# A dilated 3x3 convolution: scheduler-made streams replaced by hand-written engine streams, with a loop on TensorE

## The chip, the cores and the metric

The kernel runs on one core of a Trainium2 chip. The metric is the device time of one execution in microseconds (us): 127.39 us before the change, the median of three runs (127.07, 127.39 and 127.62 us).

## The reference

Each of 16 images has 64 input channels of 64 x 64 pixels and gives 128 output channels of the same size. The kernel is 3 x 3 with dilation 2 and zero padding of 2:

```python
for kh in range(3):
    for kw in range(3):
        output[b, co] += weight[co, ci, kh, kw] * \
            x_pad[b, ci, kh*2 : kh*2 + 64, kw*2 : kw*2 + 64]   # summed over ci
```

Input and output are 32-bit floats: 16.8 MB are read and 33.6 MB are written.

## The kernel before, in words

**Pairs and groups.** Two images (a pair) lie on 128 partitions, 64 channels each, so there are 8 pairs. A pair is worked on in 4 groups of 16 image rows, 32 groups in all, counted by `G`. TensorE multiplies each image with its own 64 rows of the array, so every product is issued twice (`hb`), once for each half.

**Fewer products.** Dilation 2 makes rows of equal `(row // 2) % 2` share terms. For a group, VectorE first adds neighbouring row pairs (`rowsum`, line 85, into `xs`). TensorE then makes three results in PSUM, each of 1024 numbers for each of 128 output channels: `psP`, the middle row of weights on the sums (6 matmuls and 6 weight loads), and `psA` and `psB`, with differences of weights on the single rows (12 each). ScalarE copies `psP` to SBUF (`p_sb`, line 233). VectorE adds `psA + p_sb` and `psB + p_sb` into the output tile `osb` (line 240). So a group has 30 matmuls, one copy, two adds and one row sum, and ScalarE also casts one chunk of the input from 32 to 16 bits (line 73).

**Weights.** At the start the weights are loaded, cast and subtracted on three engines, turned by matmuls against an identity (line 124), and copied to `w_sb`. Dummy matmuls on zeros (line 101) fill TensorE's waits there.

**Transfers.** All of them are issued on SyncE's queue (SP), one after another: weights (line 88), inputs by pair (line 64, 2 MB for a pair), outputs (lines 185 and 191, 4 MB for a pair). SyncE waits in order: a transfer whose data or buffer isn't ready holds all behind it. The order is: weights, pair 0 in two parts, pairs 1, 2, 3, then stores of pair 0, loads of pairs 4 and 5, stores of pair 1, load 6, stores of pair 2, load 7 in two parts, then stores only. Each transfer is divided over the core's 16 DMA engines. There are three input buffers, three 16-bit input buffers, three output buffers, one PSUM buffer for `psP` and three shared by `psA` and `psB`.

**One store is cut unevenly.** In the last pair, 256 KB of one store go out as 124 partitions and 4 partitions (`FOUR`), where the others have 128.

**Order and waits.** The code is written in program order, and the framework (in its manual schedule) keeps that order on each engine and puts in the semaphores. All loops are unrolled: TensorE's stream has 2009 instructions in the built program (each matmul counted with its weight load).

Of the kernel before, what the change touches and what calls it, by code (L numbers as in the profile page):

```python
# [10 lines left out]
def kernel(  # L11
# [31 lines left out]
    XF = 3  # L43

    wpool = ctx.enter_context(tc.tile_pool(name="wpool", bufs=1))
    fpool = ctx.enter_context(tc.tile_pool(name="fpool", bufs=XF))
    xpool = ctx.enter_context(tc.tile_pool(name="xpool", bufs=3))
    sxpool = ctx.enter_context(tc.tile_pool(name="sxpool", bufs=2))
    opool = ctx.enter_context(tc.tile_pool(name="opool", bufs=3))
    spool = ctx.enter_context(tc.tile_pool(name="spool", bufs=3))  # L50
    ppool = ctx.enter_context(tc.tile_pool(name="ppool", bufs=1, space=bass.MemoryType.PSUM))
    apool = ctx.enter_context(tc.tile_pool(name="apool", bufs=3, space=bass.MemoryType.PSUM))
# [4 lines left out]
    ctx.enter_context(tc.manual_schedule())  # L57

    x32_tiles, x16_tiles, xs_tiles, o_tiles = {}, {}, {}, {}

    def load(pb, cuts=(0, H)):
        x32_tiles[pb] = fpool.tile([P, HW], f32, tag="x32", name="x32")
        for lo, hi in zip(cuts[:-1], cuts[1:]):
            nc.sync.dma_start(  # L64
                out=x32_tiles[pb][:, lo * W : hi * W], in_=x_pair[pb, :, lo * W : hi * W]
            )

    def cast(c):
        pb, g = divmod(c, NG)
        lo, hi = chunk_rows[g]  # L70
        if g == 0:
            x16_tiles[pb] = xpool.tile([P, HW], f16, tag="x16", name="x16")
        nc.scalar.copy(  # L73
            out=x16_tiles[pb][:, lo * W : hi * W], in_=x32_tiles[pb][:, lo * W : hi * W]
        )

    def rowsum(c):
        pb, g = divmod(c, NG)
        if g == 0:
            xs_tiles[pb] = sxpool.tile([P, HW // 2], f16, tag="xs", name="xs")  # L80
        v = x16_tiles[pb][:, g * GR * W : (g + 1) * GR * W].rearrange(
            "p (b e q) -> p b e q", e=2, q=2 * W
        )
        s = xs_tiles[pb][:, g * NH : (g + 1) * NH].rearrange("p (b q) -> p b q", q=2 * W)
        nc.vector.tensor_tensor(out=s, in0=v[:, :, 0], in1=v[:, :, 1], op=add)  # L85

    w32 = wpool.tile([CO, CI * KH * KW], f32, name="w32")
    nc.sync.dma_start(out=w32, in_=weight.rearrange("o i h w -> o (i h w)"))  # L88
    load(0, (0, 2 * GR + d, H))
    load(1)  # L90
    load(2)
    zero = wpool.tile([P, 512], f16, name="zero")
    nc.vector.memset(zero, 0.0)  # L93
    ident = wpool.tile([P, P], f16, name="ident")
    make_identity(nc, ident)

    dm = ppool.tile([P, 2 * NH], f32, tag="p", name="dm")

    def dummies(n):
        for _ in range(n):  # L100
            nc.tensor.matmul(out=dm[:, 0:512], lhsT=zero[:, 0:P], rhs=zero)  # L101

    KINDS = 5
    NT = KINDS * KW
    wd = wpool.tile([CO, NT * CI], f16, name="wd")
    wdv = wd.rearrange("o (k j i) -> o k j i", k=KINDS, j=KW)
    wv = w32.rearrange("o (i h w) -> o h w i", h=KH, w=KW)
    w_sb = wpool.tile([P, NT * CO], f16, name="w_sb")

    dummies(6)  # L110
    nc.vector.tensor_copy(out=wdv[:, 0], in_=wv[:, 1])  # L111
    nc.gpsimd.tensor_tensor(out=wdv[:, 3], in0=wv[:, 0], in1=wv[:, 1], op=sub)  # L112
    nc.scalar.copy(out=wdv[:, 2], in_=wv[:, 0])  # L113
    nc.vector.tensor_tensor(out=wdv[:, 1], in0=wv[:, 2], in1=wv[:, 1], op=sub)
    nc.gpsimd.tensor_copy(out=wdv[:, 4], in_=wv[:, 2])  # L115

    wts = [apool.tile([P, 1024], f32, tag="ab", name="wt") for _ in range(3)]

    def turn(k):
        c0 = k // 3 * 512  # L120
        for j in range(KW):
            t = k * KW + j
            for r in range(2):
                nc.tensor.matmul(  # L124
                    out=wts[k % 3][r * CI : (r + 1) * CI, c0 + j * CO : c0 + (j + 1) * CO],
                    lhsT=wd[:, t * CI : (t + 1) * CI],
                    rhs=ident,
                )
        return w_sb[:, k * KW * CO : (k + 1) * KW * CO], wts[k % 3][:, c0 : c0 + KW * CO]

    x16_tiles[0] = xpool.tile([P, HW], f16, tag="x16", name="x16")
    t0 = turn(0)
    dummies(2)
    nc.vector.tensor_copy(out=t0[0], in_=t0[1])
    t1 = turn(1)
    nc.scalar.copy(out=t1[0], in_=t1[1])  # L136
    t2 = turn(2)
    nc.vector.tensor_copy(out=t2[0], in_=t2[1])  # L138
    dummies(1)
    t3 = turn(3)  # L140
    t4 = turn(4)
    dummies(1)
    nc.vector.tensor_copy(
        out=x16_tiles[0][:, 8 * W : 18 * W], in_=x32_tiles[0][:, 8 * W : 18 * W]
    )
    nc.scalar.copy(out=x16_tiles[0][:, 0 : 8 * W], in_=x32_tiles[0][:, 0 : 8 * W])  # L146
    nc.scalar.copy(out=t3[0], in_=t3[1])
    nc.vector.tensor_copy(out=t4[0], in_=t4[1])
    rowsum(0)

    ahead = [1]

    def casts(G):
        for n in range(2 if G else 3):
            c = ahead[0]
            if c >= ngroups or c > G + (7 if c < 2 * NG else 5):
                return
            cast(c)
            ahead[0] += 1

    def product(ps, src, kind, blk0, nblk, first, last):
        for j in (1, 0, 2):
# [3 lines left out]
            for hb in range(2):  # L166
# [4 lines left out]
                nc.tensor.matmul(  # L171
# [5 lines left out]
                )  # L177

    def blocks(x16, b0, n, e):
        v = x16.rearrange("p (b e r w) -> p b e r w", e=2, r=2, w=W)  # L180
        return lambda pp, c0, c1: v[pp, b0 : b0 + n, e, :, c0:c1]

    def store(pb, m, r0=0, r1=H, rows=((0, P),)):
        for lo, hi in rows:
            nc.sync.dma_start(
                out=out_img[2 * pb + m, lo:hi, r0 * W : r1 * W],
                in_=o_tiles[pb][lo:hi, m * HW + r0 * W : m * HW + r1 * W],
            )

    def store_both(pb, r0, r1):  # L190
        nc.sync.dma_start(
            out=out_img[2 * pb : 2 * pb + 2, :, r0 * W : r1 * W].rearrange("m o q -> o m q"),
            in_=o_tiles[pb].rearrange("p (m q) -> p m q", m=2)[:, :, r0 * W : r1 * W],
        )

    FOUR = ((0, P - 4), (P - 4, P))
    ROWS4 = 8

    for G in range(ngroups):
        pb, g = divmod(G, NG)  # L200
        x16 = x16_tiles[pb]
        xs = xs_tiles[pb].rearrange("p (r w) -> p r w", w=W)
        if g == 0:
            o_tiles[pb] = opool.tile([P, 2 * HW], f32, tag="osb", name="osb")
        o = o_tiles[pb].rearrange("p (m b e q) -> p m b e q", m=2, e=2, q=2 * W)
        b0 = g * NBLK

        def summed():
            ps = ppool.tile([P, 2 * NH], f32, tag="p", name="psP")
            sv = lambda pp, c0, c1: xs[pp, g * GR // 2 : (g + 1) * GR // 2, c0:c1]  # L210
            product(ps, sv, 0, 0, NBLK, True, True)
            return ps

        if G:
            psP = summed()

        psA = apool.tile([P, 2 * NH], f32, tag="ab", name="psA")
        product(psA, blocks(x16, b0, NBLK, 1), 1, 0, NBLK, True, False)
        z = 1 if g == 0 else 0
        product(psA, blocks(x16, b0 + z - 1, NBLK - z, 1), 2, z, NBLK - z, False, True)  # L220

        psB = apool.tile([P, 2 * NH], f32, tag="ab", name="psB")
        product(psB, blocks(x16, b0, NBLK, 0), 3, 0, NBLK, True, False)
        z = 1 if g == NG - 1 else 0
        product(psB, blocks(x16, b0 + 1, NBLK - z, 0), 4, 0, NBLK - z, False, True)

        if not G:
            psP = summed()

        if not G:  # L230
            casts(0)
        p_sb = spool.tile([P, 2 * NH], f32, tag="psb", name="p_sb")
        nc.scalar.copy(out=p_sb, in_=psP)  # L233
        if G:
            casts(G)
        if G + 1 < ngroups:
            rowsum(G + 1)
        pv = p_sb.rearrange("p (m b q) -> p m b q", m=2, q=2 * W)
        for e, ps in ((0, psA), (1, psB)):
            nc.vector.tensor_tensor(  # L240
                out=o[:, :, b0 : b0 + NBLK, e],
                in0=ps.rearrange("p (m b q) -> p m b q", m=2, q=2 * W),
                in1=pv,
                op=add,
            )

        if G == 0:
            load(XF)
        if g == NG - 1 and 0 < pb < npairs - XF - 1:
            load(pb + XF + 1, (0, H) if pb < 3 else (0, H // 2, H))  # L250
# [14 lines left out]
        elif g == NG - 1:  # L265
            store(pb, 0)
            store(pb, 1)

# [33 lines left out]
```

## Time and profile before

| | us |
|---|---|
| median of three runs | 127.39 |
| span of the profiled execution, first to last instruction | 125.1 |
| TensorE busy (share of the span) | 104.6 (84%) |
| VectorE busy | 91.0 (73%) |
| ScalarE busy | 65.0 (52%) |
| the transfers of SyncE's queue, as a share of 16 DMA engines' span | 96.5% |
| last matmul row starts | 106.65 |
| last add starts | 108.08 |

The profile is of one execution. Its span is 2.3 us shorter than the median of the runs; the page gives no other time for that execution. The page lists busy time by engine, then the span in 40 equal slices of 3.13 us, then the DMA queues (`q1` carries the kernel's transfers, `q8` fetches of instructions), the chain of work that ended last, and the costliest groups of instructions with the mean time of one and what they waited for. The issues of transfers have their own list: how often, how many KB, and the median time from issue to landing. The trace also holds a record of every DMA packet with its queue, start, size and duration.

### The profile page before, as it was taken

To read this page: it belongs to the slowest core of one execution; us is meant where nothing else is said; L and a number is where in the kernel's file an instruction comes from. 1 tells how busy PE (TensorE), PEld (TensorE's weight loads), DVE (VectorE), ACT (ScalarE), POOL (GpSimd) and SP (SyncE) were. 2 spreads that over 40 slices of the span, in tenths; PEclk is the share of its full clock that TensorE was granted. 3 is DMA by queue.
4 is the path that set the end of the run, shared out by engine and by line. 5 is a ranking of instruction groups with operands and counts; after the bars stand their busy time and mean duration, and the time that the engine had idled before them with its cause. 6 is when DMAs were issued, how large, how long until landed. Compare 5 with 4: busy or idle time off the path is not lost.

```text
span 125.1 us, 2339 instructions
## 1 busy us (share of the span) xinstructions
PE 104.6 (84%) x1000; PEld 56.7 (45%) x1000; DVE 91.0 (73%) x103; ACT 65.0 (52%) x68; POOL 2.2 (2%) x8
## 2 busy tenths in 40 slices
PE   6885999999999999999999999999999999500000
PEld 2342555555555555555555555555555555200000
DVE  0652998988898889888988898887988988700000
ACT  4377896665666566656665666566653333100000
POOL 2400000000000000000000000000000000000000
PEclk9999999999999999999999999999999999965555
DMA  4999999999999999999999999999999999999981
GB/s 123 389 457 430 435 430 419 377 430 397 438 434 430 367 424 424 432 445 419 435 419 404 417 445 435 430 430 435 424 424 424 430 424 440 430 409 411 428 379 66
DMA packets 4594, 50.78 MB, mean 406 GB/s; under 512 B 488, under 2 KB 488, under 8 KB 1256
## 3 DMA queue, kind: packets, MB, share of 16 engines
q1 hardware_dynamic: 4584, 50.63, 96.5%
q8 instruction: 8, 0.13, 0.4%
q14 instruction: 2, 0.02, 0.0%
HBM read 17.07 MB, written 33.55 MB: 405 GB/s over the span
## 4 chain that ended last, share of the span: by engine, by line
PE 76%; DMA 6%; ACT 2%; DVE 1%; DVEq 1%; SPq 1%; issue 0%
PE psA L171 31%; PE psB L171 30%; PE psP L171 16%; DMA x<-in_x_dram 6%; ACT x L73 2%; DVE osb L240 1%; DVEq L300 1%; ACT p_sb L233 1%; SPq L64 0%; SPq L88 0%; DVEq L240 0%
## 5 line engine op out<-in xcount | busy, mean ns | idle before, releaser
L171 PEld LDWEIGHTS <-w_sb 64*128 64x128 f16 x960 | 54.6, 94 | 46.3 <-issue 1.6
L233 ACT COPY p_sb<-psP 128x1024 f32<-128x1024 f32 x32 | 32.4, 1012 | 36.6 <-issue 21.5
L240 DVE TENSOR_TENSOR osb<-psA,p_sb 128x1024 f32<-128x1024 f32 x32 | 39.2, 1225 | 13.5 <-PE psA L171 9.4
L171 PE MATMUL psA<-x,w_sb 64*128 64x496 f16 (+3 forms) x384 | 45.1, 365 | 0.5 <-ACT x L146 0.5
L171 PE MATMUL psB<-x,w_sb 64*128 64x496 f16 (+3 forms) x384 | 45.1, 365 | 0.0
L240 DVE TENSOR_TENSOR osb<-psB,p_sb 128x1024 f32<-128x1024 f32 x32 | 39.1, 1222 | 0.0
L73 ACT CAST x<-x 128x1024 f16<-128x1024 f32 (+2 forms) x31 | 32.1, 1044 | 0.7 <-DMA x<-in_x_dram 0.7
L171 PE MATMUL psP<-xs,w_sb 64*128 64x496 f16 (+1 forms) x192 | 26.0, 371 | 1.3 <-ACT p_sb L233 1.3
L85 DVE TENSOR_TENSOR xs<-x 128x512 f16<-128x512 f16 x32 | 13.3, 416 | 0.7 <-ACT x L73 0.7
L101 PE MATMUL dm<-zero 128*128 128x512 f16 x10 | 4.1, 533 | 1.2 <-DVE zero L93 1.2
L111 DVE CAST wd<-w 128x192 f16<-128x192 f32 x1 | 0.5, 506 | 2.6 <-DMA w<-in_weight_dram 2.6
L101 PEld LDWEIGHTS <-zero 128*128 128x128 f16 x10 | 1.0, 121 | 2.6 <-DVE zero L93 1.2
L124 PEld LDWEIGHTS <-wd 128*64 128x64 f16 x30 | 1.0, 118 | 1.9 <-DVE wd L111 1.3
L124 PE MATMUL wt<-ident,wd 128*64 128x128 f16 x30 | 1.5, 239 | 0.4 <-DVE wd L111 0.4
L113 ACT ACT_TABLE_LOAD x1 | 1.3, 1283 | 0.7 <-PEq L286 0.7
L113 ACT CAST wd<-w 128x192 f16<-128x192 f32 x1 | 0.5, 543 | 1.7 <-DMA w<-in_weight_dram 1.7
L136 ACT CAST w_sb<-wt 128x384 f16<-128x384 f32 x1 | 0.5, 479 | 1.4 <-PE wt L124 1.4
L93 DVE MEMSET zero<- 128x256 uint32 x1 | 0.3, 272 | 0.9 <-PEq L286 0.9
L146 ACT CAST x<-x 128x512 f16<-128x512 f32 x1 | 0.6, 618 | 0.5 <-DMA x<-in_x_dram 0.5
L138 DVE CAST w_sb<-wt 128x384 f16<-128x384 f32 x1 | 0.6, 558 | 0.4 <-PE wt L124 0.4
L112 POOL TENSOR_TENSOR wd<-w 128x192 f16<-128x192 f32 x1 | 0.8, 798 | 2.5 <-DMA w<-in_weight_dram 2.5
L115 POOL CAST wd<-w 128x192 f16<-128x192 f32 x1 | 0.8, 806 | 0.0
(11 smaller groups left out, 3.8 us busy)
## 6 DMA issues: line engine op xcount, KB each, us to landing
out_dram<-osb SPq DMA_DIRECT2D x12, 2048.0 KB, 18.4
x<-in_x_dram SPq DMA_DIRECT2D x6, 2048.0 KB, 16.3
out_dram<-osb SPq DMA_DIRECT2D x4, 1024.0 KB, 13.8
out_dram<-osb SPq DMA_DIRECT2D x2, 1536.0 KB, 12.1
x<-in_x_dram SPq DMA_DIRECT2D x2, 1024.0 KB, 19.4
x<-in_x_dram SPq DMA_DIRECT2D x1, 1088.0 KB, 5.5
x<-in_x_dram SPq DMA_DIRECT2D x1, 960.0 KB, 7.3
out_dram<-osb SPq DMA_DIRECT2D x1, 768.0 KB, 15.5
```

The source lines that it names most:

```text
L73: nc.scalar.copy(out=x16_tiles[pb][:, lo * W : hi * W], in_=x32_tiles[pb][:, lo * W : hi * W])
L85: nc.vector.tensor_tensor(out=s, in0=v[:, :, 0], in1=v[:, :, 1], op=add)
L101: nc.tensor.matmul(out=dm[:, 0:512], lhsT=zero[:, 0:P], rhs=zero)
L112: nc.gpsimd.tensor_tensor(out=wdv[:, 3], in0=wv[:, 0], in1=wv[:, 1], op=sub)
L113: nc.scalar.copy(out=wdv[:, 2], in_=wv[:, 0])
L115: nc.gpsimd.tensor_copy(out=wdv[:, 4], in_=wv[:, 2])
L124: nc.tensor.matmul(out=wts[k % 3][r * CI : (r + 1) * CI, c0 + j * CO : c0 + (j + 1) * CO], lhsT=wd[:, t * CI : (t + 1) * CI], rhs=ident,)
L138: nc.vector.tensor_copy(out=t2[0], in_=t2[1])
L171: nc.tensor.matmul(out=po, lhsT=w_sb[pp, t * CO : (t + 1) * CO], rhs=rhs, start=first and j == 1, stop=last and j == 2,)
L233: nc.scalar.copy(out=p_sb, in_=psP)
L240: nc.vector.tensor_tensor(out=o[:, :, b0 : b0 + NBLK, e], in0=ps.rearrange("p (m b q) -> p m b q", m=2, q=2 * W), in1=pv, op=add,)
L300: with _tile.TileContext(nc) as tc:
```

## The change

The kernel is rewritten without the framework's scheduler: each engine's stream is written out, with its own semaphores, inside one critical section (`tile_critical`). The arithmetic, the tiling, the 32 groups and the sizes of the instructions stay. What differs:

- **TensorE loops.** The 120 matmuls of a pair are the body of a hardware loop that runs 8 times (`Fori`), with its head placed at slot 0 of an instruction block (`head_slot`). In the built program the body has 120 matmuls with their weight loads, 8 waits, one register addition and one branch: 250 instructions. Before the loop stand the 40 dummy and turning matmuls. TensorE's stream has 185 instructions in the built program, where a matmul counts once.
- **Waits of the loop.** Before each `psP` product TensorE waits for the row sum (`s_sum`), and before each `psA` product for the first add of the group before (`s_addA`); each wait takes one off the semaphore. PSUM has four slots of equal size, given out in turn (`slot`).
- **Order in group 0.** `psP` comes first there too; before, it came last.
- **Buffers.** One 16-bit input buffer where there were three, one `xs`, four input buffers where there were three. ScalarE casts chunk `G + 2` after the copy of group `G`.
- **Transfers.** The order on SyncE is the same. Load 3 no longer waits for a buffer. Load 6 goes out in two halves, and the store with 124 + 4 partitions and its neighbour of 768 KB are one plain store again.
- **The frame around it.** SyncE runs a no-operation and a branch that waits for it before the first transfer, and the other engines wait for it too. At the end GpSimd waits for all stores and clears the semaphores, SyncE gathers all engines, and then comes the framework's own closing part as before.

The core of the diff:

```diff
-    XF = 3
...
-    xpool = ctx.enter_context(tc.tile_pool(name="xpool", bufs=3))
-    sxpool = ctx.enter_context(tc.tile_pool(name="sxpool", bufs=2))
...
-    ppool = ctx.enter_context(tc.tile_pool(name="ppool", bufs=1, space=bass.MemoryType.PSUM))
-    apool = ctx.enter_context(tc.tile_pool(name="apool", bufs=3, space=bass.MemoryType.PSUM))
+    XF = 4
+    OF = 3
+    PF = 3
...
-    ctx.enter_context(tc.manual_schedule())
+    ctx.enter_context(tc.tile_critical())
+    pe, act, dve, pool, sp = nc.tensor, nc.scalar, nc.vector, nc.gpsimd, nc.sync
...
+    slots = [nc.alloc_psum_tensor(f"ps_{i}", [P, 2 * NH], f32).ap() for i in range(4)]
+
+    def slot(G, i):
+        return slots[(3 * G + i) % 4]
...
+    cast(1)
+    for G in range(ngroups):
+        act.wait_ge(s_pe.s, 3 * G + 1)
+        copy_n[G] = s_act.by(act.copy(out=psb[G % PF], in_=slot(G, 0)))
+        cast(G + 2)
...
+    def take(c):
+        pe.wait_ge(c.s, 1).then_inc(c.s, -1)
+
+    pe.wait_ge(s_act.s, w_ready)
+    PE = mybir.EngineType.PE
+    with nc.Fori(0, npairs, engines=[PE], head_slot={PE: 0}):
+        for g in range(NG):
+            b0 = g * NBLK
+            take(s_sum)
+            s_pe.by(product(slot(g, 0), sums(g), 0, 0, NBLK, True, True))
+            take(s_addA)
+            product(slot(g, 1), blocks(b0, NBLK, 1), 1, 0, NBLK, True, False)
+            z = 1 if g == 0 else 0
+            s_pe.by(product(slot(g, 1), blocks(b0 + z - 1, NBLK - z, 1), 2, z, NBLK - z, False, True))
+            product(slot(g, 2), blocks(b0, NBLK, 0), 3, 0, NBLK, True, False)
+            z = 1 if g == NG - 1 else 0
+            s_pe.by(product(slot(g, 2), blocks(b0 + 1, NBLK - z, 0), 4, 0, NBLK - z, False, True))
...
+    for G in range(ngroups):
...
+        rowsum(G + 1)
+        dve.wait_ge(s_act.s, copy_n[G])
+        if g == 0 and pb >= OF:
+            dve.wait_ge(s_store[pb - OF].s, stored(pb - OF))
+        for e, c in ((0, s_addA), (1, s_addB)):
+            dve.wait_ge(s_pe.s, 3 * G + 2 + e)
...
-                if g == 1:
-                    store(pb, 1, 0, 2 * GR - ROWS4)
-                    store(pb, 1, 2 * GR - ROWS4, 2 * GR, FOUR)
...
+    done(NG - 2)
+    store(0, 0, 0, (NG - 1) * GR)
+    store(0, 1, 0, (NG - 1) * GR)
+    done(NG - 1)
+    store_both(0, (NG - 1) * GR, H)
+    more(XF)
+    for pb in range(1, npairs - 1):
+        if pb + XF < npairs:
+            more(pb + XF, (0, H) if pb < 2 else (0, H // 2, H))
+        done(NG * pb + NG - 1)
+        store(pb, 0)
+        store(pb, 1)
+    pb = npairs - 1
+    for g in (1, NG - 1):
+        done(NG * pb + g)
+        store(pb, 0, (g - 1) * GR, (g + 1) * GR)
+        store(pb, 1, (g - 1) * GR, (g + 1) * GR)
+    for pb in range(npairs):
+        pool.wait_ge(s_store[pb].s, s_store[pb].n)
+    nc.clear_and_free_semaphores(sems)
```

`done(G)` makes SyncE wait for the second add of group `G`; `more(pb)` makes it wait for the last cast out of the buffer that the load reuses.

## The prediction

> **What bounds the kernel now.** I read first the busy shares and the slices, then the DMA queues and the issues, then the stages, and last the chain.
>
> ```profile
> PE 104.6 (84%) x1000; PEld 56.7 (45%) x1000; DVE 91.0 (73%) x103; ACT 65.0 (52%) x68; POOL 2.2 (2%) x8
> ...
> PE   6885999999999999999999999999999999500000
> ...
> DMA  4999999999999999999999999999999999999981
> ...
> q1 hardware_dynamic: 4584, 50.63, 96.5%
> q8 instruction: 8, 0.13, 0.4%
> ...
> out_dram<-osb SPq DMA_DIRECT2D x12, 2048.0 KB, 18.4
> ```
>
> TensorE looks like the bound: 84%, and 9s from slice 5 on. But its row ends in slice 35, and the DMA row has 9s from slice 2 to slice 38. A 2 MB store takes 18.4 us to land; its 128 packets of 16 KB, 8 on each of 16 DMA engines at 0.61 us (the usual duration in the packet records), need 4.9 us. The other 13.5 us it lies in the queue behind others. The stages say the same:
>
> ```profile
> 72.00:96.00 24.00, 24.00 (x236) 13.26 (x234) 21.11 (x25) 14.15 (x15) 0.00 (x0) 1.00 1.01 431
> 96.00:108.00 12.00, 11.95 (x116) 6.38 (x112) 10.27 (x11) 4.05 (x4) 0.00 (x0) 1.00 1.00 426
> 108.00:119.00 11.00, 0.00 (x0) 0.00 (x0) 1.30 (x2) 0.00 (x0) 0.00 (x0) 0.61 1.00 421
> ```
>
> The last two columns are the DMA share and GB/s. From 108 to 119 us no matmul runs and the transfers go on at 421 GB/s, as before. The chain of waits gives TensorE 76%, but it ends in a TensorE-and-VectorE path that is done at 109 us; it does not follow the stores. **The transfers are the bound**: 50.63 MB at 429 GB/s (16 x 16 KB in 0.61 us) are 118.0 us, from the first packet at 1.75 us on, so a perfect queue would end at 119.8 us. The records end at 123.9 us. The gap is partly slow packets (2.0 us on each engine, on average, above the usual duration of their size), and partly unevenness: the sixteen engines end between 120.1 and 123.9 us, as the taper shows (0.65 us per entry from 100 us on, GB/s):
>
> ```profile
> GB/s 429 403 403 504 403 454 429 429 429 403 429 403 454 479 378 403 391 429 441 403 416 429 410 403 413 422 444 416 451 432 429 353 340 265 176 88 13 0 0 0
> ```
>
> Then 1.16 us follow until the span ends at 125.07 us.
>
> **How far compute is ahead.** From the records, by issue and the first packet of that store on any engine: the first stores of pair 0 are issued at 19.63 us and begin at 22.70; those of pair 6 at 96.95 and 101.13; the last at 109.32 and 115.16. TensorE can be late by 3.1, 4.2 and 5.8 us there before a DMA engine runs dry.
>
> **The change, part by part.** All sums are made against the profiled span, 125.07 us; what lies around it, 127.39 - 125.07 = 2.32 us by the median, I leave as it is.
>
> *Bytes and order.* The same 50.63 MB go out in the same order. Load 3 is issued some 8 us earlier (it waits until about 11 us now), but its first packet starts at 17.6 us behind loads 1 and 2: 0. Load 6 in halves: a packet of 8 KB takes 0.309 us, two of them 0.618 for 0.611: 0.
>
> *TensorE's new wait.* `psA` of a group now needs the first add of the group before. Before, `psB` did, 1.27 us later.
>
> ```profile
> 63.20 1.45 PE L171 MATMUL psB<-x,w_sb 64*128 64x512 f16 x12
> 63.49 1.23 DVE L240 TENSOR_TENSOR osb<-psA,p_sb 128x1024 f32<-128x1024 f32 x1 [0.41 <-PE psA L171]
> ...
> 65.11 1.45 PE L171 MATMUL psA<-x,w_sb 64*128 64x512 f16 x12
> ```
>
> The add ends at 64.72, `psA` begins at 65.11: 0.39 us to spare. Queued behind the wait are this group's 24 `psA` and `psB` products and the next row of groups; VectorE and the stores wait for them. VectorE keeps its order (row sum, first add, second add), 0.42 + 2 x 1.23 = 2.87 us of a group's 3.17 (61.30 to 64.47 from one `psP` to the next), so it does not fall behind, and I take 0. If the cover went and each wait cost 0.1 us, 32 groups lose 3.2 us, still under the margin of 4.2. `psP` needs a row sum that is done 1.4 us earlier (62.66 + 0.42 against 64.47): 0. Casting into the one 16-bit buffer follows the copy of group `G`, which itself follows all of group `G - 1`, the last reader: no new wait. Cast and copy are 1.05 + 1.01 of 3.17 us.
>
> *Order in group 0.* `psP` first waits for the row sum, at about 8.0 us where `psA` starts at 7.34 now. But the 1.29 us that TensorE now waits for the copy at 11.8 us goes, because the other slot is free: group 1 starts at about 8.05 + 0.64 + 1.27 + 1.27 = 11.2 to 11.3 us instead of 11.82. TensorE gains 0.5 us, hidden.
>
> *The loop.* 7 back edges. The trace has no branch inside the work. Bounds: 0, if the queue of issued matmuls covers it; 3.0 us each, the longest thing like a fetch here (the weights' 288 KB take 3.0 us from issue to landing). A fetch's own packet takes 0.93 us (8 of 16 KB on q8 in 7.4 us). I take under 0.5 us each, nearest to the packet, as part of it lies beside issued matmuls: 7 x 0.5 = 3.5 us on TensorE, less the 0.5 gained; at pair 6 (6 edges) 2.5 us of the 4.2. On the path: 0.
>
> [...]
>
> *Fetches.* Unrolled, TensorE draws 8 blocks during the work, on seven different DMA engines (one gets two), 0.93 us each. In a loop they go. *The uneven store.* 124 + 4 partitions run on four engines, 32 packets of 2 KB each, 80 ns apart (2.57 us), nothing on the other twelve; a plain store puts 8 on each (0.64 us). In the records the four end at 122.9 to 123.9 us, the twelve at 120.1 to 123.4. So plain: the four end by 122.0, the twelve up to 0.64 later, at most 124.1: +0.17. Take the fetches off as well (seven of eight fell on the twelve, two on the latest of them): the last is then 122.9, **-1.0 us**. The other end: the latest engine had no fetch and gets 0.64 more: **+0.65**. Which engine has had the slow packets is chance here (they come at 21 to 23 and 41 to 43 us, up to 1.7 us for 0.61), so I take half of the gain: **-0.5**.
>
> *The frame.* Start: one no-operation and one more branch before the first transfer. SyncE goes from its released wait to the first issue in 0.08 us now (0.66 to 0.74), with one branch: 0 to 0.15, I take **+0.1**. End: the closing part today:
>
> ```profile
> L300 SPq EVENT_SEMAPHORE  x7: 17/28/28, 118.9 to 125.0; - x7
> L300 POOLq EVENT_SEMAPHORE  x4: 17/17/17, 124.4 to 125.0; - x4
> ...
> L300 POOLq EVENT_SEMAPHORE_RANGE_CLEAR  x1: 96/96/96, 124.7 to 124.7; - x1
> ```
>
> From SyncE's last wait (124.26) two gatherings of all engines take 0.81 us. The change puts ahead of that a drain and a clear on GpSimd (0.31 us for drain, clear and drain now, 124.58 to 124.89), a hop to SyncE (0.05) and branches (0.08): 0.3 to 0.8, I take **+0.45**. All of it comes after the last byte; nothing hides it.
>
> Sum: -0.5 + 0.1 + 0.45 = +0.05 us, a span of 125.1 and a time of **127.4 us**. The ends: -1.0 + 0 + 0.3 = -0.7 (126.7) and +0.65 + 0.15 + 0.8 = +1.6 (129.0).
>
> **The rivals.**
>
> *The fetches were what made the tail late* (faster). For: one late engine had two of them. Against: the slow packets at 21 and 41 us cost more and stay. The full -1.0 with the cheap frame: 126.7 us. Chance 0.22.
>
> *The tail gets worse* (slower). The uneven store was a counterweight; without it the twelve get 0.64 more, no fetch falls on the latest, and the frame costs 0.5: 127.4 + 1.15 = 128.55 us. Chance 0.20.
>
> *The loop's edges stall TensorE until the stores come late* (slower). The place is the branch back, the price is that of a fetch, and it decides from (4.2 + 0.5) / 6 = 0.78 us per edge, where the stores of pair 6 find dry engines. At 0.95 us an edge: 6 x 0.95 - 4.7 = 1.0 us, 128.4. At 3.0 us: TensorE ends at about 128.4 us, the add 1.35 later, two stores of 1 MB 4.9 us, 1.0 to the first packet, 1.6 of closing: span 137.3, time 139.6. [...] Chance 0.10.
>
> **How the numbers follow.** The forecast has 0.48, the rivals 0.22, 0.20 and 0.10. A measurement here tells about 0.5% (0.64 us) from no change: faster means below 126.75, slower above 128.03. The forecast lies within; so 0.22, 0.48, 0.30. The range takes in both ends of the sum and the runs' own scatter (0.3 us): 126.4 to 129.2. The stall at 3 us is left out.
>
> **What would show it.** q8 falls from 8 packets to 3 or fewer; q1 stays at 96% or more; TensorE ends by 112 us with gaps of under 0.5 us every 12.4 us; no idle before `psA` on VectorE; the first transfer is issued at about 0.84 us; the span ends about 1.6 us after the last packet. Wrong would be DMA slices under 9 between 20 and 120 us, or engines that end more than 4 us apart.

## The result

| | before | after |
|---|---|---|
| median of four executions each, us | 127.23 (126.59 to 127.62) | 128.41 (128.29 to 128.65) |
| span of the profiled execution, us | 125.07 | 126.88 |
| first packet of a transfer starts, us | 1.75 | 1.96 |
| last packet ends, us | 123.92 | 125.12 |
| from there to the end of the span, us | 1.15 | 1.76 |

The changed kernel is **slower by 1.2 us**: ratio 1.0105, 95% interval 1.006 to 1.015. The forecast was 127.4 us and, as the likeliest case, no difference that can be measured. The time lies inside the range that was given, but the likeliest case is not what came: slower had a chance of 0.30. An execution more than 1.5% above the fastest of its kernel counts as slow here; the ratios leave those out and are no quotients of the medians, while the medians and lowest spans take all. Later executions list span and time side by side: 1.7 to 1.9 us as a rule lie around the span, not the 2.3 that the prediction took from the median. The profiled execution of the kernel before was thus one of about 126.9 us. So the spans of the two profiles lie 1.8 us apart and the medians 1.2.

### The profile page after: what moved, and what is told of

The parts are those of the page before. It is cut to its first block, busy times and chain, and to the rows that moved or that the text cites. A ratio compares the mean times of both kernels' runs of the same rounds, so it can differ in the third digit from the quotient of the medians.

```text
span 126.9 us, 2394 instructions
## 1 busy us (share of the span) xinstructions
PE 104.5 (82%) x1000; PEld 56.6 (45%) x1000; DVE 91.0 (72%) x103; ACT 64.9 (51%) x68; POOL 2.2 (2%) x8
## 3 DMA queue, kind: packets, MB, share of 16 engines
q1 hardware_dynamic: 4592, 50.63, 95.2%
## 5 line engine op out<-in xcount | busy, mean ns | idle before, releaser
L285 DVE TENSOR_TENSOR osb<-ps,psb 128x1024 f32<-128x1024 f32 x64 | 76.8, 1223 | 13.7 <-PE ps L224 12.5
L224 PE MATMUL ps<-x,w_sb 64*128 64x496 f16 (+3 forms) x768 | 84.4, 365 | 0.6 <-PEq L242 0.6
L224 PEld LDWEIGHTS ps<-x,w_sb 64*128 64x128 f16 x768 | 43.7, 94 | 36.5 <-issue 2.3
L210 ACT COPY psb<-ps 128x1024 f32<-128x1024 f32 x32 | 32.4, 1013 | 37.5 <-PE ps L224 37.5
L224 PE MATMUL ps<-xs,w_sb 64*128 64x496 f16 (+1 forms) x192 | 26.0, 371 | 1.6 <-PEq L242 1.6
L224 PEld LDWEIGHTS ps<-xs,w_sb 64*128 64x128 f16 x192 | 10.9, 94 | 10.3 <-issue 1.9
L133 PE MATMUL ps<-zero 128*128 128x512 f16 x10 | 4.1, 533 | 1.4 <-DVE zero L169 1.4
L133 PEld LDWEIGHTS ps<-zero 128*128 128x128 f16 x10 | 1.0, 122 | 2.8 <-DVE zero L169 1.4
L144 PE MATMUL ps<-ident,wd 128*64 128x128 f16 x30 | 1.4, 223 | 0.4 <-DVE wd L171 0.4
L175 DVE CAST w_sb<-ps 128x384 f16<-128x384 f32 x2 | 1.1, 550 | 0.4 <-PE ps L144 0.4
```

Source lines behind the costliest of these rows:

```text
L133: pe.matmul(out=dm[:, 0:512], lhsT=zero[:, 0:P], rhs=zero)
L144: m = pe.matmul(out=ps[r * CI : (r + 1) * CI, j * CO : (j + 1) * CO], lhsT=wd[:, t * CI : (t + 1) * CI], rhs=ident,)
L175: dve.tensor_copy(out=turned(k)[0], in_=turned(k)[1])
L210: copy_n[G] = s_act.by(act.copy(out=psb[G % PF], in_=slot(G, 0)))
L224: m = pe.matmul(out=po, lhsT=w_sb[pp, t * CO : (t + 1) * CO], rhs=rhs, start=first and j == 1, stop=last and j == 2,)
L285: dve.tensor_tensor(out=o[:, :, b0 : b0 + NBLK, e], in0=slot(G, 1 + e).rearrange("p (m b q) -> p m b q", m=2, q=2 * W), in1=pv, op=add,)
```

## The profile after

From the page of the changed kernel: busy shares, the slices of TensorE and of the transfers, the queues, and the issues (KB each, us from issue to landing).

```profile
PE 104.5 (82%) x1000; PEld 56.6 (45%) x1000; DVE 91.0 (72%) x103; ACT 64.9 (51%) x68; POOL 2.2 (2%) x8
...
PE   5849999999999999999999999998999999200000
...
DMA  4999999899999999999999999999999999999930
...
q1 hardware_dynamic: 4592, 50.63, 95.2%
q8 instruction: 1, 0.02, 0.0%
...
out_dram<-osb SPq DMA_DIRECT2D x12, 2048.0 KB, 19.7
```

TensorE, VectorE and ScalarE are busy for as long as before, within 0.1 us, and the transfers fill the slices from 2 on as before, but for one 8 at 22 to 25 us. A store lands 1.3 us later (18.4 before). Only one fetch of 16 KB is left on `q8`. Stretch by stretch (busy time of each engine; the last two columns are the DMA share and GB/s) the transfers keep their pace as well:

```profile
72.00:96.00 24.00, 23.42 (x229) 12.73 (x227) 20.31 (x24) 15.01 (x16) 0.00 (x0) 1.00 1.02 433
96.00:108.00 12.00, 12.00 (x119) 6.61 (x116) 10.22 (x12) 5.84 (x6) 0.00 (x0) 1.00 1.00 429
108.00:119.00 11.00, 0.54 (x8) 0.12 (x3) 1.90 (x2) 0.00 (x0) 0.00 (x0) 0.76 1.00 423
```

433, 429 and 423 GB/s stand where 431, 426 and 421 stood. Nothing was lost in the middle. The tail is different: GB/s from 100 us on, 0.65 us per entry, as shown of the kernel before.

```profile
GB/s 429 504 403 479 454 403 479 403 403 403 403 403 429 429 403 529 429 378 391 441 416 441 416 416 429 416 429 429 416 441 416 441 391 126 50 50 50 38 13 0
```

Before, the rate fell in steps (353, 340, 265, 176, 88, 13): the engines ended one after another between 120.1 and 123.9 us. Now it falls at once from 391 to 126 and then stays at 50, 50, 50, which is two engines of sixteen (one moves about 27 GB/s: 16 KB in 0.61 us). Each engine's share of a transfer ends with a record of 4 bytes, its completion record (496 of them here, sixteen for each of 31 transfers). By these, fourteen engines end between 121.3 and 122.2 us, one at 124.4 and one at 125.1. **The mean of the last sixteen records is not later (122.33 us before, 122.18 now), but the last one is.**

The loop costs nothing that the end sees. TensorE's branches at the loop's line, with the least, median and greatest ns:

```profile
L246 PEldq COMPARE_BRANCH  x9: 76/208/298, 8.2 to 106.3; - x9
```

Nine branches of at most 0.30 us, and no fetch lies in the loop's seven passes back: the one on `q8` is at 12.6 us, in the first pass. VectorE and TensorE in the steady state (start, us, the last bracket is idle time before and what ended it):

```profile
63.33 2.42 DVE L285 TENSOR_TENSOR osb<-ps,psb 128x1024 f32<-128x1024 f32 x2 [0.42 <-PE ps L224]
64.31 0.81 PE L224 MATMUL ps<-xs,w_sb 64*128 64x512 f16 x6
64.94 2.72 PE L224 MATMUL ps<-x,w_sb 64*128 64x512 f16 x24
```

The `psA` and `psB` products follow `psP` without idle time, so the new wait on the first add costs nothing there. From one `psP` to the next are 3.17 us, as before (64.31, then 67.48).

The frame, first the start. SyncE's issue of the weights in the kernel before:

```profile
0.74 0.38 SPq L88 DMA_DIRECT2D w<-in_weight_dram  x1
```

and in the changed one, 0.20 us later:

```profile
0.94 0.38 SPq L92 DMA_DIRECT2D w<-in_weight_dram  x1
```

At the end, GpSimd's drain and clear of 29 semaphores, and SyncE's no-operation that follows them (ns, and the start in us):

```profile
L338 POOLq DRAIN  x1: 105/105/105, 125.7 to 125.7; - x1
L338 POOLq EVENT_SEMAPHORE_RANGE_CLEAR  x1: 200/200/200, 125.8 to 125.8; - x1
...
L52 SPq NOP  x2: 13/13/13, 0.7 to 126.1; - x2
```

The last packet ends at 125.12 us, the no-operation is at 126.1, and only then come the framework's two gatherings, until 126.88. What follows the last packet differs between kernels: 1.15 and 1.16 us in the two profiles of the kernel before, 1.35 and 1.41 in those of its two variants, 1.62 to 1.76 in the changed kernel and its variants with the same end.

## Experiments

**The theories.** *Theory*: the loss is the frame (0.2 us at the start, 0.4 to 0.6 at the end) and the missing uneven store, which relieved one DMA engine that stores more slowly than the others. *Rival 1*: it is the frame, and chance in the tail. *Rival 2*: the loop. *Rival 3*: the fetches were worth a good part of the tail. Each kernel ran in five rounds beside the kernel before on the same chip, whose medians were 126.78 to 126.80 us (127.50 beside the last). A ratio is against that. "After" is the changed kernel. The profile of the one with uneven store and short end is of one of its slowest executions (span 128.1 us).

The table gives also the lowest span of each kernel, because single executions of a kernel differ by 2 us and more and their lower end repeats well: for the kernel before it was 124.7 us on each of the four chips, and 124.5 in its second set on one of them. The other kernels have 6 to 12 executions each, the kernel before 11 to 23 on a chip; drawn from its spans, the lowest of 6 would be about 0.1 us higher (an estimate), so differences of 0.1 to 0.2 us in this column say little.

| kernel | median, us | ratio (95% interval) | lowest span, us | last packet in the profile |
|---|---|---|---|---|
| before | 126.78 | | 124.7 | 123.92 |
| before again | 127.53 | 1.0007 (0.9964 to 1.0049) | 124.5 | 124.56 |
| before, plain store | 127.43 | 1.0036 (1.0000 to 1.0072) | 125.2 | 124.09 |
| before, load 4 first | 127.00 | 1.0006 (0.9982 to 1.0030) | 124.8 | 124.91 |
| after, again | 129.05 | 1.0137 (1.0081 to 1.0193) | 126.4 | 124.90 |
| after, uneven store | 128.19 | 1.0099 (1.0066 to 1.0131) | 125.9 | 125.55 |
| after, unrolled | 129.30 | 1.0179 (1.0125 to 1.0232) | 126.5 | 124.76 |
| after, 120 + 8 rows | 131.83 | 1.0382 (1.0330 to 1.0433) | 129.4 | 128.53 |
| after, short end | 128.80 | 1.0100 (1.0041 to 1.0160) | 126.1 | 125.96 |
| after, loads as before | 129.38 | 1.0149 (1.0086 to 1.0213) | 126.6 | 125.71 |
| after, uneven and short end | 128.21 | 1.0071 (1.0027 to 1.0115) | 125.6 | 126.86 |
| after, load 4 first | 128.56 | 1.0144 (1.0100 to 1.0188) | 126.3 | 124.68 |
| after, loads 4 and 5 first | 131.60 | 1.0247 (1.0176 to 1.0318) | 128.0 | 129.90 |

**1. The uneven store, put back into the changed kernel.**

```diff
-        store(pb, 1, (g - 1) * GR, (g + 1) * GR)
+        if g == 1:
+            store(pb, 1, 0, 2 * GR - 8)
+            store(pb, 1, 2 * GR - 8, 2 * GR, ((0, P - 4), (P - 4, P)))
+        else:
+            store(pb, 1, (g - 1) * GR, (g + 1) * GR)
```

> The changed kernel with only the uneven store put back (256 KB of the last pair as 124 + 4 partitions, on four DMA engines). Theory (the loss is the frame, 0.8 us, plus the missing counterweight: one DMA engine, not among the four, has packets of 0.64 for 0.61 us and ends last): that engine gets 0.64 us less work, so 127.8 us where the changed kernel has 128.4, with the last packet about 0.6 us earlier. Rival 1 (all of the loss is the frame and chance in the tail): 128.4, no change. Rival 2 (the loop): 128.4, no change.

The ratio is 1.0099 where the changed kernel has 1.0105 and 1.0137: between the theory and rival 1, and not to be told from either. The lowest span is 125.9 us against 126.4, 0.5 less. In its profile the tail ends in steps again, though in this execution, of 127.2 us, the last packet (125.55) is not the 0.6 us earlier that was expected (GB/s from 100 us on):

```profile
GB/s 504 454 403 429 429 429 403 403 479 454 429 403 403 403 429 529 403 403 429 403 391 366 454 432 400 425 419 403 441 425 429 457 429 366 277 252 151 76 38 0
```

**2. The plain store in the kernel before**, the same edit from the other side.

```diff
-                if g == 1:
-                    store(pb, 1, 0, 2 * GR - ROWS4)
-                    store(pb, 1, 2 * GR - ROWS4, 2 * GR, FOUR)
-                else:
-                    store(pb, 1, (g - 1) * GR, (g + 1) * GR)
+                store(pb, 1, (g - 1) * GR, (g + 1) * GR)
```

> The kernel before with only the uneven store replaced by a plain one. Theory: the slow DMA engine gets 0.64 us more and ends last, 127.8 to 127.9 us where the kernel before has 127.2; the frame stays as it was (first issue at 0.74 us, 1.2 us from the last packet to the end). Rival 1 and rival 2: 127.2, no change.

Ratio 1.0036 (1.0000 to 1.0072), lowest span 125.2 against 124.7: again 0.5 us. Both sides give the same size, so the uneven store acts as a counterweight, worth about 0.5 us; the medians alone would leave 0 to 0.9. Part of it may lie behind the last packet, where this profile has 1.41 us, not the 1.2 expected.

**3. The loop written out.**

```diff
-    with nc.Fori(0, npairs, engines=[PE], head_slot={PE: 0}):
+    for _ in range(npairs):
```

> The changed kernel with TensorE's loop written out eight times; waits, order and frame unchanged. Theory (the loop is hidden and the fetches hit engines that have room): q8 goes from 1 packet to about 7, TensorE ends within 1 us of where it did, and the time stays at 128.4 (128.2 to 128.9, later by up to 0.6 us if a fetch falls on the slow engine). Rival 2 (the loop costs, by its branch and by the 1.6 us wait ahead of its first product): 127.8 or less. Rival 3 (the fetches were worth a good part of the tail): 129.0 or more.

The fetches are back, from the page of this kernel:

```profile
q8 instruction: 7, 0.11, 0.3%
```

Its lowest span is 126.5 us, that of the changed kernel is 126.4: rival 2 falls, as the loop isn't the loss, and by the span so does rival 3. The sixteen engines end 0.5 us later on average (122.68 against 122.18 and 122.01), of which 7 fetches make an estimated 0.4 (at 0.93 us each, the mean of the eight in the kernel before, on 16 engines), but the last one doesn't (124.76 against 125.12 and 124.90): **in this profile no fetch falls on the engine that ends last** from 49 us on, as its lag grows by no more than 0.3 us a store. The median of 129.30 misses the theory's 128.2 to 128.9 and would fit rival 3 (129.0 or more). But it is only 0.25 us over that of the changed kernel on the other chip, with intervals that overlap, and this kernel has more time around the span (2.2 us in the middle; see the last section), which an effect on the tail doesn't explain.

**4. 120 + 8 rows in one store of the last pair**, meant to find out which engine is the slow one.

```diff
-        store(pb, 1, (g - 1) * GR, (g + 1) * GR)
+        store(pb, 1, (g - 1) * GR, (g + 1) * GR, ((0, 120), (120, P)) if g == 1 else ((0, P),))
```

> The changed kernel with one 1 MB store of the last pair issued as 120 + 8 partitions, so that, if a transfer of 120 partitions is divided over 15 engines as one of 124 was over four, the sixteenth engine has none of it (2.45 us less) and the first eight have 0.31 us more. Theory, if the slow engine is the sixteenth: the last packet comes 0.7 (then the second latest engine ends last) to 2.4 us earlier, 126.0 to 127.7 us. If the slow engine is one of the other fifteen, and for rivals 1 and 2: 128.4 to 128.7.

A miss: 3 us slower than the changed kernel. 8 KB packets after 112 us, 0.309 us each in the other kernels with plain stores (none over 0.33), take up to 1.02 us here, at 115 to 122.5 us, and cost 0.9 us on each engine on average. It tells nothing of which engine is slow.

**5. and 6. Both kernels as they are**, as a yardstick and for a second profile.

> The changed kernel as it is, beside the kernel before on this chip, as the yardstick for the other kernels here. Theory (frame 0.8 us, missing counterweight 0.46, loop -0.9, and some 0.8 us not yet explained): ratio 1.0105 as in the first comparison, 1.2 to 1.3 us. Rival, chance of that chip or those runs: a ratio of under 1.006. In the profile: first transfer issued at 0.94 us, span ends 1.5 to 1.8 us after the last packet, the engine with the 0.64 to 0.67 us packets ends last.

> The kernel before as it is, for a second profile of it. What it is to tell: the last packet was at 123.92 us and the slow DMA engine at about 123.2 us in the one profile so far, and the kernels of the changed form end 0.8 to 1.2 us later than their edits account for. If that is the kernels' own, this profile shows a last packet at 123.5 to 124.3 us; if it was chance of one profile, one at over 124.6 us. Ratio 1.000 within 0.003.

The loss repeats: 1.0137. The second profile of the kernel before has its last packet at 124.56 us, between the two forecasts (124.3 and 124.6), so it settles nothing alone. The second one of the changed kernel is like the first in all that counts: fourteen engines end by 122.1 us, the last two at 124.4 and 124.9.

**7. A shorter end.**

```diff
-    ctx.enter_context(tc.tile_critical())
+    ctx.enter_context(tc.tile_critical(no_gpsimd_drain=True))
...
-    for pb in range(npairs):
-        pool.wait_ge(s_store[pb].s, s_store[pb].n)
-    nc.clear_and_free_semaphores(sems)
+    s_done = Count("s_done")
+    s_done.by(sp.nop())
+    last = s_store[-1]
+    pool.wait_ge(s_done.s, 1)
+    for c in s_store[:-1]:
+        pool.wait_ge(c.s, c.n)
+    nc.clear_and_free_semaphores([s for s in sems if s is not last.s])
+    pool.wait_ge(last.s, last.n).then_inc(last.s, -last.n)
```

> The changed kernel with a shorter end: GpSimd clears all semaphores but that of the last pair's stores as soon as the earlier stores have landed, and after the last pair's stores it only waits and counts that one semaphore down; the section's own drain of GpSimd is left out. Theory (the end frame costs 0.4 to 0.6 us, read from the end of the span): 0.3 to 0.5 us faster than the changed kernel, 128.0 against 128.4 us, and 1.76 us after the last packet become 1.25 to 1.45. Rival (the end frame is hidden behind something else at the end, and what is late is in the transfers): no difference, within 0.1 us.

The clears are now done long before the end:

```profile
L342 POOLq EVENT_SEMAPHORE_RANGE_CLEAR  x2: 44/114/183, 116.8 to 117.1; - x2
```

From the last packet to the end of the span are 1.37 us instead of 1.62 to 1.76. The lowest span falls by 0.3 us and the median by 0.25 (128.80 against 129.05; the intervals of the two ratios overlap): the end frame is on the path, as the theory has it. The 0.2 us of the start were not taken away by a run; they are read from the first issue.

**8. The loads as before**: load 3 held back until pair 0 is cast, load 6 whole.

```diff
-    for pb in range(1, XF):
+    for pb in range(1, XF - 1):
...
+    sp.wait_ge(s_act.s, cast_n[NG - 1])
+    load(XF - 1)
     done(NG - 2)
...
-            more(pb + XF, (0, H) if pb < 2 else (0, H // 2, H))
+            more(pb + XF, (0, H) if pb < 3 else (0, H // 2, H))
```

> The changed kernel with its loads as before: load 3 is held back until pair 0 is cast, and load 6 is one transfer of 2 MB instead of two halves. Theory A (the 0.8 us not yet explained lie in the earlier and halved loads, which put more slow packets at the change from loads to stores): 0.6 to 1.0 us faster than the changed kernel, 127.6 us. Theory B (the loads lie behind others in any case, priced at 0 in the forecast): no difference, within 0.2 us.

No gain (lowest span 126.6 us, median 129.38, against 126.4 and 129.05): theory B, the forecast's 0 for the loads holds.

**9. Uneven store and short end together** (the edits of 1 and 7).

> The changed kernel with the uneven store of the kernel before put back and the end shortened as in the lean kernel. In the undisturbed executions so far the spans were 124.7 to 125.0 us for the kernel before, 126.4 to 126.7 for the changed one, 125.9 to 126.1 with the uneven store, 126.1 to 126.3 with the short end. Theory (counterweight 0.5 and end frame 0.35 are two separate terms): they add up, 125.6 us of span at the low end and 127.3 to 127.6 us, still 0.7 above the kernel before. Rival (both act on the same last engine): the second adds nothing, 125.9 or more.

Lowest span 125.6 us, as the sum has it: 0.5 and 0.3 are two terms. The median of 128.21 is above the forecast of 127.3 to 127.6. It still loses to the kernel before (1.0071): of 0.9 us in lowest spans the start has 0.2 and the end about 0.1 (1.25 us behind the last packet instead of 1.15), so about 0.6 us lie somewhere else.

**10. and 11. Load 4 ahead of pair 0's stores**, in both kernels, so that the engines change from loads to stores later.

```diff
+    more(XF)
-    done(NG - 2)
-    store(0, 0, 0, (NG - 1) * GR)
-    store(0, 1, 0, (NG - 1) * GR)
     done(NG - 1)
-    store_both(0, (NG - 1) * GR, H)
-    more(XF)
+    store(0, 0)
+    store(0, 1)
```

> The changed kernel with load 4 issued before pair 0 is stored, and pair 0 stored whole after its last group like the other pairs, so that the DMA engines go from loads to stores once later, at about 27 us, and in larger pieces. It asks whether the part of the loss not in the frame and not in the counterweight (about 0.5 us of a later last packet) comes from where the first stores meet the loads: packets at 18 to 26 us were 0.63 to 0.87 us per engine over their usual time in the changed kernel's profiles and 0.04 to 0.35 in those of the kernel before. Theory (it is that meeting): the excess at 18 to 26 us falls under 0.1 us and the low end of the spans goes from 126.5 to 126.0 us, the time to 127.9. Rival (the excess only moves to the next change of direction): 126.5 us or more, 128.4.

> The kernel before with the same edit: load 4 before the stores of pair 0, which go out whole. Theory (the meeting of first stores and loads decides): little to gain here, since its excess at 18 to 26 us is 0.04 to 0.35 us: 126.5 to 126.8 us, at best a version that beats both kernels by 0.2. Rival (excess only moves): within 0.2 us of the kernel before, or up to 0.5 slower where the first change of direction falls later.

The slow packets do move: at 18 to 26 us the excess falls from 0.87 and 0.63 us per engine to 0.09, and at 26 to 36 us it rises from 0.03 to 0.82. The lowest spans change by 0.1 us (126.3, 124.8), the ratios not measurably. That is the rival: the excess only moves.

**12. Loads 4 and 5 first**, the same step once more.

```diff
     more(XF)
+    more(XF + 1)
     done(NG - 1)
     store(0, 0)
     store(0, 1)
     for pb in range(1, npairs - 1):
-        if pb + XF < npairs:
-            more(pb + XF, (0, H) if pb < 2 else (0, H // 2, H))
         done(NG * pb + NG - 1)
         store(pb, 0)
         store(pb, 1)
+        if pb < 3:
+            more(pb + XF + 1, (0, H // 2, H))
```

> The changed kernel with loads 4 and 5 both ahead of pair 0's stores, pairs 0 and 1 stored in one row and load 6 behind them, so that the DMA engines go from loads to stores first at about 33 us. In the completions of the transfers one engine drifts away from the others by 0.25 us per 2 MB store and ends 2.9 us behind the mean in the changed kernel, 2.6 with load 4 first (its packets over their usual time fell at 26 to 36 us instead of 18 to 26). Theory (the later the packets over their usual time fall, the more of them the drifting engine is spared, and so the earlier the end): excess at 33 to 40 us, the drifting engine ends 2.0 to 2.4 us behind the mean, low end of the spans 126.0 us against 126.5 (changed) and 126.3 (load 4 first), 127.9 us. Rival (the place doesn't matter, and what is 0.5 us later than in the kernel before has another cause): low end 126.3 to 126.6, 128.3 us.

A miss by its own wait. SyncE holds load 5 until pair 1 is cast, and pair 0's stores, ready at about 26 us, stand behind it in the queue (the issues in this kernel's profile, which is of its slowest execution):

```profile
17.27 12.70 SPq L98 DMA_DIRECT2D x<-in_x_dram  x2
30.02 9.01 SPq L303 DMA_DIRECT2D out_dram<-osb  x4
```

Load 4 runs out before that, and the transfers stand still (GB/s from 20 to 40 us, 0.5 us per entry); from 26 to 36 us the DMA share is 0.73, a loss of 2.7 us:

```profile
GB/s 426 328 524 426 459 426 361 426 492 459 426 426 328 492 459 164 33 33 0 0 0 360 164 131 295 393 426 459 360 459 393 229 393 98 492 393 328 360 524 492
```

Its last engine ends 4.2 us behind the mean, not 2.0 to 2.4, so the theory that a later change spares the slow engine gets no support. But the profile shows the drift cleanly, as after the standstill no other engine is late. From the completion records (each of the sixteen engines writes 4 bytes when its share of a transfer is done), the last engine's lag behind the mean of the sixteen, at successive 2 MB stores:

```
mean completion, us    37.4   42.3   47.1   52.0   56.9  ...  106.0  110.9
last engine behind     0.63   0.78   1.04   1.32   1.57  ...   4.01   4.19
```

**One engine loses about 0.25 us on each 2 MB store**: its 16 KB packets of a store take 0.64 to 0.67 us instead of 0.61, eight of them a store. Why that engine is slower is not shown, and the trace has no engine's number.

The same view of the other kernels, the last and the last but one of sixteen successive completions behind their mean, in us (one of the last sixteen can be a late engine's transfer before the last, which moves the column on the right by about 0.1):

| | at about 48.7 us | at about 73 us | at about 98 us | at the end |
|---|---|---|---|---|
| before, plain store | 2.09, 1.86 | 1.74, 1.51 | 1.51, 1.29 | 1.56, 1.35 |
| after, unrolled | 1.75, 0.59 | 1.53, 1.23 | 1.74, 1.30 | 2.08, 1.14 |
| after | 2.22, 0.52 | 2.52, 1.32 | 2.58, 2.42 | 2.95, 2.27 |
| after, again | 2.45, 0.50 | 2.58, 1.24 | 2.53, 2.53 | 2.89, 2.36 |

In the changed kernel the second value climbs from 0.5 to 2.4: the drifting engine overtakes one that was late early and ends last. That the early lateness comes from the fetch at 12.6 us (0.99 us long in the first profile) and the first stores is likely, but not shown. Fetches raise the mean by 0.4 in the upper two rows (an estimate: 7 or 8 of 0.93 us on 16 engines), so there the end is 2.0 and 2.5 by the measure of the lower two. The drifting engine thus ends 0.5 to 0.9 us nearer to the others in the kernel before.

Most of this is there by 54 us. The engine can be followed by its packets of 0.64 to 0.67 us. It completes the second store of pair 1 at 53.2 us in the kernel before and at 53.4 with the plain store, but at 54.3 and 54.1 in the two profiles of the changed kernel; the start explains 0.2 us of that. From there to its completion at 104 to 105 us all of them need 50.8 to 51.0 us. Yet the second profile of the kernel before has 54.3 us there too, so single profiles don't tell what belongs to the kernel and what to the execution.

## Why the prediction was right or wrong

- **The bound** (the transfers) was right: writing out the loop, which adds fetches and takes the branches away, moved the lowest span by 0.1 us, and the DMA share stays at 1.00 from 108 to 119 us, where TensorE is done.
- **The loop** (7 edges under 0.5 us, hidden: 0) was right: nine branches of 0.08 to 0.30 us, and unrolled the lowest span is the same within 0.1 us (126.5 against 126.4). The rival that the edges stall TensorE is out.
- **The new wait** (0) was right, as the lines at 63 to 65 us show. **Order in group 0**: its first product starts at 8.65 us (8.0 forecast) and group 1 at 11.66 (11.2 to 11.3 forecast, 11.82 before), hidden. **Loads** (0): right, by experiment 8.
- **Not foreseen** was a wait of VectorE for an output buffer, because a store lands 1.3 us later:

```profile
85.91 2.35 DVE L285 TENSOR_TENSOR osb<-ps,psb 128x1024 f32<-128x1024 f32 x2 [1.18 <-DMA out_dram<-osb]
```

  TensorE then has a gap of 0.58 us at 87.28. Both are hidden: the DMA share of that stretch, 72 to 96 us, is 1.02.
- **The frame**: start +0.2 us, forecast +0.1 (bounds 0 to 0.15, so above the upper one); end +0.6 in the profiles, forecast +0.45 (0.3 to 0.8), of which the short end took back 0.3. Mechanism right, sizes a little small: +0.8 instead of +0.55 by the two profiles. Between the two kernels with plain stores the end differs by 0.35 (1.41 and 1.76 us behind the last packet).
- **Fetches and uneven store, -0.5 us: this is the step that failed.** It took half of a gain of 1.0 on the thought that the four engines with the uneven store would end earlier and that fetches had fallen on the others. The runs put +0.5 for the plain store (experiments 1, 2 and 9) and 0 for the fetches (experiment 3) in its place. "Which engine has had the slow packets is chance" was wrong: besides the slow packets that come by chance, one engine is slower store by store (16 KB in 0.64 to 0.67 us instead of 0.61), in the profiles of the kernel before as in those of the changed one. That it isn't among the four is inferred from the relief; no record names an engine. The prediction's upper end, +0.65, was that case.
- **The rivals.** "The tail gets worse" (128.55 us, chance 0.20) names what came: the counterweight, no fetch on the latest engine, a dearer frame. It should have been the forecast. That its time is so near to the 128.41 us measured is luck in part: 0.4 to 0.7 us of the loss (next point) have no place in its sum. The record that tells it was in the trace of before: the lag of each completion, and the 65 packets of 16 KB at 0.64 to 0.67 us that stand one behind the other.
- **The sum.** In lowest spans the kernels lie 1.7 us apart (124.7, 126.4). 0.2 (start), 0.3 to 0.6 (end) and 0.5 (store) make 1.0 to 1.3. **0.4 to 0.7 us stay open**: the drifting engine ends nearer to the others in the kernel before, also without the uneven store. It isn't the loop, the fetches, load 3 or load 6, nor the place of the first stores. In the profiles before, the slow packets by chance lie at 36 to 48 us (0.51, 0.84 and 1.14 us per engine), in the changed kernel's two at 18 to 26 (0.87, 0.63). This goes with the execution more than with the kernel: four variants of the changed kernel (uneven store, short end, both, loads as before) have 0.63 to 1.11 us at 36 to 48 too. In these the drifting engine lies 0.2 us ahead of the mean to 0.1 behind it at 49 to 55 us, as in the kernel before and its plain variant (0.45 ahead to 0.3 behind), against 0.5 to 0.8 behind in the changed kernel's two. So where the slow packets fall goes with how far back that engine is, but it doesn't explain why the lowest spans differ.
- **What would show it**: `q8` at one packet, TensorE done by 108.5 us and the span's end 1.76 us after the last packet (about 1.6 forecast) came about as told, and so did the idle time of VectorE in the steady state (0.42 us, as before). Not as told were the 1.18 us of VectorE above, TensorE's gap of 0.58 us, `q1` at 95.2% instead of 96, and the first issue at 0.94 instead of 0.84. Of the two signs of error no slice between 20 and 120 us shows more than the usual dip (one 8, at 22 to 25 us), while the engines end 3.8 us apart (121.3 to 125.1), just under the 4 named.

No version here beats the kernel before.

## What to carry to other kernels

Here transfers were the bound (DMA share 1.00 from 108 to 119 us, with TensorE done by 108.5), and the last of sixteen DMA engines decided the end: 125.1 us in the changed kernel, where fourteen were done by 122.2. In such a kernel look at how far each completion lies behind the mean before calling an uneven transfer or a fetch a cost. An edit that looks like clumsiness, such as a store on four engines, may be the counterweight of a slower engine, like the one here that lost about 0.25 us on each 2 MB store; the uneven store was worth 0.5 us of lowest span in both kernels. And the drain and clear behind the last byte were on the path here, worth 0.3 us of lowest span: they can be done for all semaphores but the last transfer's while that transfer is still under way.

## What the runs showed of the hardware

**Fetches behind the end.** In 10 of 63 executions of the looped kernels the time is 2.5 to 3.0 us over the span instead of 1.7 to 2.0; in 108 executions of the kernel before and its two variants it was never over 1.95. The second profile of the changed kernel is of such an execution (129.20 us, span 126.7): it has a fetch of 16 KB at 128.48 us, 0.96 us long, after the span's end. The unrolled kernel's profile has one at 127.52 us, 1.40 us long (128.68 us, span 126.5). Only one of the ten has a profile, so that a fetch is the cause in all of them is not shown.

**The same matmuls at two paces.** From 8 to 12 us the changed kernel's first profile (busy us of TensorE first, with its number of matmuls in brackets; the last three numbers are the granted clock, the DMA share and GB/s):

```profile
8.00:12.00 4.00, 3.35 (x34) 1.96 (x36) 2.10 (x5) 2.96 (x4) 0.00 (x0) 1.00 1.05 448
```

and the kernel with the short end, in which nothing differs at that place:

```profile
8.00:12.00 4.00, 3.46 (x19) 1.31 (x17) 1.31 (x3) 2.59 (x4) 0.00 (x0) 1.00 1.04 446
```

34 and 19 matmuls in as much busy time, and the granted clock is 1.00 in both. The first stores of the second are issued at 22.4 us instead of 19.5; that its slower start is the reason is likely, but not shown. Leaving out the kernels whose stores were moved or cut in 120 + 8 rows, the profiles with late first stores (21.2 to 22.6 us) have 2.3 to 3.4 us per engine of packets over their usual time, those with early ones 1.8 to 2.2. Such differences are between executions of one kernel as well, and are larger than what this change does.
